# Gated DeltaNet on one core: another order of z, the convolutions, the inverse and the heads

## The chip, the core and the metric

The kernel runs on one core of a Trainium2 chip. The number is the device time of one execution in microseconds (us). Five engines work side by side, each through its own queue in order: PE (TensorE, matmuls and transposes; PEld is its weight load), DVE (VectorE), ACT (ScalarE), POOL (GpSimd) and SP (SyncE, which here issues the loads of weights). Operands lie in SBUF, PE writes to PSUM.

## The reference

Two layers on 256 tokens of 1024 numbers, all in float32. The change touches the mixer of the first layer, a gated DeltaNet with 8 heads of 128:

```python
x = x + 0.5 * swiglu(rmsnorm(x, ffn1_norm[layer]), ...)
x = x + mixer(rmsnorm(x, mix_norm[layer]))
x = x + 0.5 * swiglu(rmsnorm(x, ffn2_norm[layer]), ...)

proj = h @ w_in                      # q, k, v, z (1024 columns each), b, a
qkv = silu(causal_depthwise_conv(qkv, w_conv))        # 4 taps
q, k = l2norm(q) * DK ** -0.5, l2norm(k)
beta, g = sigmoid(b), -exp(A_log) * softplus(a + dt_bias)
# per head and chunk:
L = strictly_lower((k * beta) @ k.T * decay)
u, w = solve(I + L, [v * beta, k * beta * exp(g)])
o = (q * exp(g)) @ S + (q @ k.T * decay) @ (u - w @ S)
S = S * exp(g_last) + k_dec.T @ (u - w @ S)
y = (rmsnorm(o, out_norm) * silu(z)).reshape(T, H * DV) @ w_out
```

The kernel takes chunks of 128 tokens, so there are two chunks t = 0, 1. The second layer's mixer is a sliding-window attention and is not touched.

## The kernel before

**Matmuls.** Every large product of float32 numbers is done as three matmuls on parts: a weight piece `raw` of 128x1024 numbers is loaded by SP, ACT rounds it to a high part `whi` (L310), and DVE takes the low part `wlo` = raw - whi (L312), or POOL does it in four instructions of 128x256 (L317). `mm3` then makes hi x hi, hi x lo and lo x hi (L363 to L365).

**The mixer's stages** (about 195 to 370 us of the run). z, k, v and q are each projected in four chunks c of 256 columns. A chunk of z is 48 matmuls of 128x256 into PSUM buffers (`pz`, copied by ACT to `zs`). A chunk of k, v or q (`conv`) has two halves f of 128 columns: 24 matmuls `pcv` each, then ACT starts `cv` with one tap (L925), DVE adds three more from PSUM (L928), and ACT takes the silu (L932). PSUM has four buffers psA for pz, pcv and acc, four psB for the rest.

After each k chunk, `kpost` transposes k (`pkn`), sums its squares (L721) and makes k k^T (`pkk`), which DVE multiplies by the decay into `nf`. `blocks(g)` takes the 32x32 diagonal blocks of the four heads of group g, scales them by `knbr` and masks them on POOL (L768, L770). `inverse` inverts all these small triangles on DVE, from a transpose at L780 to one at L818, whose output is `yx`. `chain(g)` builds the full 128x128 inverse `yf` of each head and chunk from them, by small matmuls on PE with a copy by ACT or DVE behind each: `pt`, `py` (L833), `pt` (L853), `py` (L865), `px` (L873), `pt` (L881), `py` (L887). `state` then makes u, w and S (`puu`, `pwt`, `pS`, `pws`). `qpost` makes q k^T (`pkq`) and the squares of q (`pqn`) per q chunk. `o_of(t, g)` makes the outputs `po` of four heads, `post` normalises and gates them (ACT square L1051, DVE sum L1052, POOL power L1055, DVE product L1057 into `on`), `turn` transposes them (`poT`) and splits them into `oT` (L1068, L1069). `out_part` multiplies by w_out into `acc`, `out_add` adds to x; `after(t)` normalises x for the next FFN, whose transposes are `psT` and whose first products are `pgu`.

**The order.** The code is a program whose order is partly set by a `Ticker`: generators (gates, kpost, inverse, chain, state, ...) are advanced by one step after each f of a convolution. From that program a scheduler fixes each engine's order before the run, keeping an engine busy with what it thinks is ready, earlier code first; `issue_after` adds an order between two instructions. In the program before, z's chunks 0 to 2 come first, then k, v, q, with z's chunk 3 inside q's third; the inverse's steps and both chains go on one ticker.

Of the kernel before, what the change touches and what calls it, by code (L numbers as in the profile page):

```python
# [9 lines left out]
F32 = mybir.dt.float32  # L10
# [203 lines left out]
class Kern:  # L214
    def __init__(self, ctx, tc):
# [11 lines left out]
        self.early = None  # L227

# [59 lines left out]
    def split(self, src, hi, lo, shape, eng=None, cuts=1):  # L288
# [9 lines left out]
        with ExitStack() as behind:  # L298
# [14 lines left out]
            if eng is not None:  # L313

                r, h, l = (a.rearrange("p a b -> p (a b)").rearrange("p (n f) -> p n f", f=256) for a in (raw, hi, lo))
                for i in range(4):
                    eng.tensor_tensor(out=l[:, i], in0=r[:, i], in1=h[:, i].bitcast(F32), op=ALU.subtract)  # L317
# [10 lines left out]
    def wcols(self, w, c0, npool=0):  # L328
        src = w[:, c0:c0 + 256].rearrange("(k p) f -> p k f", p=P)
        pieces = [self.wpiece(src[:, 4 * i:4 * i + 4, :], 4, 256,  # L330
                              eng=self.nc.gpsimd if i >= 2 - npool else None) for i in range(2)]
        return lambda k, cs: tuple(a[:, k % 4, cs] for a in pieces[k // 4])
# [47 lines left out]
    def proj_T(self, out, w, f, nrm):  # L380
        fs = slice(f * P, (f + 1) * P)
        for k in range(KT):
            wh, wl = w(k, fs)
            self.mm3(out, wh, wl, nrm.h.hi(k), nrm.h.lo(k), k == 0, k == KT - 1)
# [217 lines left out]
    def gdn_gates(self, nrm, wh, wl, expA, dtb, Dt, wq, res):  # L602
# [27 lines left out]
        nc.scalar.activation(e, na, AF.Exp)  # L630
# [50 lines left out]
    def gdn(self, nrm, prep, w_in, w_out, after):  # L681
# [9 lines left out]
        tk = Ticker()  # L691
        Dt = self.big([P, NT, H, P], "Dt")
# [24 lines left out]
        def sumsq(pv, ss, h0):  # L717
            for i in range(2):
                for t in range(NT):
                    j = self.small([P, P], "junk", 1)  # L720
                    nc.scalar.activation(j, pv[:, t, i, :], AF.Square, accum_out=ss[:, t, h0 + i:h0 + i + 1])  # L721
# [3 lines left out]
        def kpost(c):  # L725
# [7 lines left out]
            beta, eG, eS = res["beta"], res["eG"], res["eS"]  # L733
# [7 lines left out]
            a = ssk[:, :, hs]  # L741
            nc.vector.tensor_scalar_add(a, a, EPS)
            nc.vector.reciprocal(br[:, :, hs], a)
            nc.vector.tensor_mul(br[:, :, hs], br[:, :, hs], beta[:, :, hs])
            nc.vector.tensor_scalar_mul(nbr[:, :, hs], br[:, :, hs], -1.0)
            yield
            nc.gpsimd.tensor_tensor(out=kd[:, hs, :], in0=kd[:, hs, :], in1=bc(eS, 0, hs), op=ALU.mult)
            nc.gpsimd.tensor_tensor(out=keg[:, hs, :], in0=keg[:, hs, :], in1=bc(eG, 1, hs), op=ALU.mult)
# [7 lines left out]
        def blocks(g):  # L756
# [4 lines left out]
            us = slice(8 * g, 8 * g + 8)  # L761
            raw = self.y1([P, 8, 32], "d32")
# [6 lines left out]
            for j, m in enumerate(("tri16", "off16")):  # L769
                nc.gpsimd.tensor_tensor(out=d2[:, j, us, :], in0=raw,  # L770
                                        in1=M[m].unsqueeze(1).to_broadcast([P, 8, 32]), op=ALU.mult)
            nc.gpsimd.tensor_tensor(out=sv[:, :, gs], in0=ssk[:, :, gs],
                                    in1=self.phalf.rearrange("p (t h) -> p t h", t=NT), op=ALU.pow)

        def inverse():
# [21 lines left out]
            yield  # L797
# [13 lines left out]
            yield  # L811
# [6 lines left out]
            nc.vector.transpose(yx[:, 1].rearrange("p u c -> p (u c)"), yx[:, 0].rearrange("p u c -> p (u c)"))  # L818
            late["yx"] = yx
            tk.add(chain(0), chain(1))  # L820

        def chain(g):
# [6 lines left out]
            def blockwise(ps, lhsT, rhs):  # L829
                for i in range(8):  # L830
                    for b in range(4):
                        bs = slice(32 * b, 32 * b + 32)
                        nc.tensor.matmul(ps[bs, i * 32:i * 32 + 32], lhsT=lhsT[bs, i, :], rhs=rhs[bs, i, :],  # L833
                                         start=True, stop=True)
# [540 lines left out]
```

## Time and profile before

| | us |
|---|---|
| median of three runs (lowest, highest) | 1017.47 (1017.03, 1020.1) |
| the profiled execution | 1017.73 |
| its span in the profile | 1016.0 |
| PE busy | 998.0 |

The profile is of one execution. A row of the waits names the engine and instruction that stood still, what released it, and the us. A row of a timeline has start, duration, engine, line, operation, output and inputs, and behind it in brackets the idle time ahead and its releaser. Groups of instructions have the count, busy us, mean ns, and idle us ahead. Windows give busy us of each engine in a stretch and the granted clock of PE (1.00 is full speed).

### The profile page before, as it was taken

To read this page: it belongs to the slowest core of one execution; us is meant where nothing else is said; L and a number is where in the kernel's file an instruction comes from. 1 tells how busy PE (TensorE), PEld (TensorE's weight loads), DVE (VectorE), ACT (ScalarE), POOL (GpSimd) and SP (SyncE) were. 2 spreads that over 40 slices of the span, in tenths; PEclk is the share of its full clock that TensorE was granted. 3 is DMA by queue.
4 is the path that set the end of the run, shared out by engine and by line. 5 is a ranking of instruction groups with operands and counts; after the bars stand their busy time and mean duration, and the time that the engine had idled before them with its cause. 6 is when DMAs were issued, how large, how long until landed. Compare 5 with 4: busy or idle time off the path is not lost.

```text
span 1016.0 us, 16483 instructions
## 1 busy us (share of the span) xinstructions
PE 998.0 (98%) x6195; PEld 870.7 (86%) x6195; DVE 643.7 (63%) x975; ACT 547.8 (54%) x979; POOL 242.1 (24%) x311
## 2 busy tenths in 40 slices
PE   8999999999989999999999999999999999999997
PEld 7888888899979888888888888888898678888886
DVE  5866654666895766666546666664578756666544
ACT  5756544457856445555434655553467545555442
POOL 0125510017952301323100123320021402222100
PEclk9999999999999999999999999999999999999999
DMA  7766666644452337666666666665563426666661
GB/s 246 235 188 191 200 197 182 205 129 148 133 175 65 105 104 208 195 188 197 191 199 190 186 187 186 192 207 189 185 209 104 152 91 212 190 189 187 203 188 43
DMA packets 135316, 177.05 MB, mean 174 GB/s; under 512 B 7250, under 2 KB 120260, under 8 KB 135236
## 3 DMA queue, kind: packets, MB, share of 16 engines
q1 hardware_dynamic: 132032, 171.46, 55.3%
q10 hardware_dynamic: 3204, 4.53, 1.4%
q8 instruction: 49, 0.80, 0.3%
q14 instruction: 31, 0.25, 0.1%
HBM read 174.92 MB, written 1.05 MB: 173 GB/s over the span
## 4 chain that ended last, share of the span: by engine, by line
PE 89%; DVE 4%; ACT 3%; issue 1%; DMA 1%; POOL 1%; SPq 1%; POOLq 0%; ACTq 0%
PE pg L370 14%; PE pu L370 14%; PE acc L365 9%; PE acc L363 9%; PE acc L364 9%; PE pu L371 7%; PE pg L371 7%; PE pgu L365 2%; PE pgu L364 2%; PE pgu L363 2%; DVE wlo L312 1%; DMA raw<-in_ffn_w_gu_dram 1%; PE pcv L363 1%; PE pcv L364 1%; PE pcv L365 1%
## 5 line engine op out<-in xcount | busy, mean ns | idle before, releaser
L312 DVE TENSOR_TENSOR wlo<-raw,whi 128x1024 fp32r<-128x1024 f32 (+1 forms) x304 | 374.9, 1236 | 198.0 <-ACT whi L310 196.8
L310 ACT CAST whi<-raw 128x1024 fp32r<-128x1024 f32 (+1 forms) x318 | 330.3, 1046 | 179.5 <-PE acc L365 83.2
L370 PE MATMUL pg<-hs,whi 128*128 128x512 f32 x624 | 218.7, 392 | 0.0
L370 PE MATMUL pu<-hs,whi 128*128 128x512 f32 x624 | 218.4, 392 | 0.0
L371 PE MATMUL pu<-hs,wlo 128*128 128x256 f32 x624 | 175.4, 281 | 0.0
L371 PE MATMUL pg<-hs,wlo 128*128 128x256 f32 x624 | 174.6, 281 | 0.0
L478 POOL TENSOR_TENSOR act<-act,gate 128x256 f32<-128x256 f32 x78 | 58.6, 751 | 352.0 <-DVE act L477 337.4
L370 PEld LDWEIGHTS pg<-hs,whi 128*128 128x128 f32 x624 | 116.9, 187 | 25.3
L370 PEld LDWEIGHTS pu<-hs,whi 128*128 128x128 f32 x624 | 116.9, 187 | 25.2
L364 PE MATMUL acc<-wlo,ah 128*128 128x512 f32 (+1 forms) x340 | 128.6, 378 | 0.0
L365 PE MATMUL acc<-whi,al 128*128 128x512 f32 (+1 forms) x340 | 128.5, 378 | 0.0
L363 PE MATMUL acc<-whi,ah 128*128 128x512 f32 (+1 forms) x340 | 128.0, 378 | 0.0
L371 PEld LDWEIGHTS pg<-hs,wlo 128*128 128x128 f32 x624 | 118.2, 189 | 0.4
L371 PEld LDWEIGHTS pu<-hs,wlo 128*128 128x128 f32 x624 | 118.2, 189 | 0.0
L363 PEld LDWEIGHTS acc<-whi,ah 128*128 128x128 f32 x340 | 64.0, 188 | 12.0
L364 PEld LDWEIGHTS acc<-wlo,ah 128*128 128x128 f32 x340 | 64.0, 188 | 11.8
L365 PEld LDWEIGHTS acc<-whi,al 128*128 128x128 f32 x340 | 64.0, 188 | 11.9
L481 POOL TENSOR_SCALAR ah<-act 128x256 fp32r<-128x256 f32 x78 | 66.4, 852 | 6.7
L467 ACT COPY gate<-pg 128x256 f32<-128x256 f32 x78 | 28.7, 368 | 55.6 <-PE pg L371 55.6
L476 ACT COPY act<-pu 128x256 f32<-128x256 f32 x78 | 28.7, 368 | 54.1 <-PE pu L371 54.1
L363 PE MATMUL pcv<-hs,whi 128*128 128x256 f32 x192 | 55.1, 287 | 2.2 <-DVE cv L928 2.2
L99 POOL TENSOR_TENSOR rst<-var,mhalf 128x1 f32<-128x1 f32 x10 | 5.6, 557 | 215.6 <-DVE var L97 215.6
(340 smaller groups left out, 1576.6 us busy)
## 6 DMA issues: line engine op xcount, KB each, us to landing
raw<-in_ffn_w_gu_dram SPq DMA_DIRECT2D x156, 512.0 KB, 4.4
raw<-in_ffn_w_down_dram SPq DMA_DIRECT2D x88, 512.0 KB, 4.2
raw<-in_a_w_in_dram SPq DMA_DIRECT2D x32, 512.0 KB, 4.2
raw<-in_ffn_w_gu_dram SPq DMA_DIRECT2D x40, 256.0 KB, 4.7
raw<-in_b_w_in_dram SPq DMA_DIRECT2D x12, 512.0 KB, 4.8
raw<-in_a_w_out_dram SPq DMA_DIRECT2D x8, 512.0 KB, 3.7
raw<-in_b_w_out_dram SPq DMA_DIRECT2D x8, 512.0 KB, 3.7
nw<-in_ffn_norm_dram ACTq DMA_DIRECT2D x3, 512.0 KB, 4.0
```

The source lines that it names most:

```text
L99: nc.gpsimd.tensor_tensor(out=r, in0=v, in1=k.mhalf[:, 0:1], op=ALU.pow)
L310: nc.scalar.copy(hi[:, c], raw[:, c])
L312: nc.vector.tensor_tensor(out=lo[:, c], in0=raw[:, c], in1=hi[:, c].bitcast(F32), op=ALU.subtract)
L363: nc.tensor.matmul(out, lhsT=lh, rhs=rh, start=start, stop=False)
L364: nc.tensor.matmul(out, lhsT=lh, rhs=rl, start=False, stop=False)
L365: return nc.tensor.matmul(out, lhsT=ll, rhs=rh, start=False, stop=stop)
L370: nc.tensor.matmul(out, lhsT=lh, rhs=r2, start=start, stop=False)
L371: return nc.tensor.matmul(out[:, :T], lhsT=ll, rhs=rh, start=False, stop=stop)
L467: nc.scalar.copy(g, pg[:, T:])
L476: nc.scalar.copy(a, pu[:, T:])
L478: nc.gpsimd.tensor_tensor(out=a, in0=a, in1=gates[f], op=ALU.mult)
L481: ahead[2] = nc.gpsimd.tensor_scalar(oh, a, 1.0, None, op0=ALU.mult)
```

## The change

z's chunks 2 and 3 move behind the k convolutions. A chunk of z and a convolution now have two PSUM accumulators open: the first four k pieces for both, then the last four for both. Each chain has a ticker of its own, advanced at every quarter of a convolution, and its matmuls are placed behind the matmuls of that quarter (`late["mm"]`). The inverse has no yields. The scaling of kd and keg goes behind the last POOL piece of v's second chunk. br and nbr are computed per group in `blocks`, the root of ssk in `roots`. Squares of k and q are one ACT instruction of 128x512 in place and one DVE sum. Of the weights of z's chunks 2 and 3 and of the k chunks 0 to 2, one piece of two gets its low part on POOL (before: none of z, 0, 0, 1, 1 for the k chunks). The outputs of heads 0 to 3 for both chunks, their post and turn come during q's convolutions (`heads`). At the end both chunks' acc are open, and the first four k pieces of both precede the turns of heads 4 to 7. z is gated in pieces of 128x256.

On DVE, the end of the inverse in the order before (cv are taps, wlo low parts of weights, yx the result):

```order
L810 TENSOR_REDUCE inv<-tw 128x8x8
L928 SCALAR_TENSOR_TENSOR cv<-pcv,wc,cv 128x255 x2
L812 COPY tw<-inv 128x512
L928 SCALAR_TENSOR_TENSOR cv<-pcv,wc,cv 128x254 x2
L815 STREAM_TRANSPOSE tw<-tw 128x16x32
L928 SCALAR_TENSOR_TENSOR cv<-pcv,wc,cv 128x253
L312 TENSOR_TENSOR wlo<-raw,whi 128x1024
L928 SCALAR_TENSOR_TENSOR cv<-pcv,wc,cv 128x253
L816 TENSOR_TENSOR yx<-tw,blk_953 128x512
L312 TENSOR_TENSOR wlo<-raw,whi 128x1024
L928 SCALAR_TENSOR_TENSOR cv<-pcv,wc,cv 128x255
L818 STREAM_TRANSPOSE yx<-yx 128x512
```

and after:

```order
L313 TENSOR_TENSOR wlo<-raw,whi 128x1024
L823 COPY tw<-inv 128x512
L951 SCALAR_TENSOR_TENSOR cv<-pcv,wc,cv 128x255
L951 SCALAR_TENSOR_TENSOR cv<-pcv,wc,cv 128x253
L826 STREAM_TRANSPOSE tw<-tw 128x16x32
L951 SCALAR_TENSOR_TENSOR cv<-pcv,wc,cv 128x254
L827 TENSOR_TENSOR yx<-tw,blk_953 128x512
L951 SCALAR_TENSOR_TENSOR cv<-pcv,wc,cv 128x255
L951 SCALAR_TENSOR_TENSOR cv<-pcv,wc,cv 128x253
L829 STREAM_TRANSPOSE yx<-yx 128x512
L951 SCALAR_TENSOR_TENSOR cv<-pcv,wc,cv 128x254
L313 TENSOR_TENSOR wlo<-raw,whi 128x1024
```

Low parts of weights stand thinner here; the taps alternate with the steps as before.

On POOL, the masked blocks ahead of the inverse, before (d are the blocks, kk the two scaled copies of k, ks the root of ssk):

```order
L770 TENSOR_TENSOR d_2607<-d_2608,tri_958 128x256
L770 TENSOR_TENSOR d_2607<-d_2608,off_967 128x256
L317 TENSOR_TENSOR wlo<-raw,whi 128x256 x4
L772 TENSOR_TENSOR ks<-ssk,phalf 128x2x4
L768 TENSOR_TENSOR d_2781<-d_2781,knbr 128x256
L770 TENSOR_TENSOR d_2607<-d_2781,tri_958 128x256
L770 TENSOR_TENSOR d_2607<-d_2781,off_967 128x256
L317 TENSOR_TENSOR wlo<-raw,whi 128x256 x12
```

and after, where the masks for the second group (d<-d,tri) are followed by the remaining scalings:

```order
L785 TENSOR_TENSOR ks<-ssk,phalf 128x2x4
L775 TENSOR_TENSOR d_2595<-d_2595,knbr 128x256
L318 TENSOR_TENSOR wlo<-raw,whi 128x256 x4
L747 TENSOR_TENSOR kk_1908<-kk_1908,gexp 128x256
L748 TENSOR_TENSOR kk_1908<-kk_1908,gexp 128x256
L747 TENSOR_TENSOR kk_1908<-kk_1908,gexp 128x256
L777 TENSOR_TENSOR d_2421<-d_2595,tri_958 128x256
L777 TENSOR_TENSOR d_2421<-d_2595,off_967 128x256
L785 TENSOR_TENSOR ks<-ssk,phalf 128x2x4
L748 TENSOR_TENSOR kk_1908<-kk_1908,gexp 128x256
```

One low part and now three scalings stand between d<-d,knbr and its masks; the root comes behind them.

On PE, what follows q's last convolution, before (py and puu are of chain and state, pkq and pqn of q):

```order
L365 MATMUL pcv<-hs,wlo 128x256
L887 MATMUL py<-yf,xa 64x64 x16
L1004 MATMUL puu<-u,yf 128x128 x8
L901 MATMUL pkq<-qT,kT 128x128 x4
L714 MATMUL pqn<-ident,qT 128x128 x4
L1004 MATMUL pwt<-yf,kk_1908 128x128 x8
L1004 MATMUL po<-u,Dt 128x128 x4
L1004 MATMUL pS<-u,kk_1908 128x128 x8
L901 MATMUL pkq<-qT,kT 128x128 x4
L714 MATMUL pqn<-ident,qT 128x128 x4
```

and after:

```order
L1039 MATMUL po<-S,wq 128x128
L1039 MATMUL po<-u,Dt 128x128
L917 MATMUL pkq<-qT,kT 128x128
L718 MATMUL pqn<-ident,qT 128x128 x2
L917 MATMUL pkq<-qT,kT 128x128 x3
L718 MATMUL pqn<-ident,qT 128x128 x2
L1103 MATMUL poT<-ident,on 128x128 x4
L365 MATMUL acc<-whi,oT 128x512
L366 MATMUL acc<-wlo,oT 128x512
```

The products of the chain and of the state that stood behind the last convolution are gone from there; po, pkq and pqn of the last q chunk and a poT are followed by acc.

```diff
-            for i in range(2):
-                for t in range(NT):
-                    j = self.small([P, P], "junk", 1)
-                    nc.scalar.activation(j, pv[:, t, i, :], AF.Square, accum_out=ss[:, t, h0 + i:h0 + i + 1])
+            nc.scalar.activation(pv, pv, AF.Square)
+            nc.vector.tensor_reduce(out=ss[:, :, h0:h0 + 2], in_=pv, axis=AX.X, op=ALU.add)
...
-            nc.scalar.copy(kd[:, hs, :], pv[:, 0])
-            nc.scalar.copy(keg[:, hs, :], pv[:, 1])
+            nc.scalar.copy(kk2[:, :, hs, :], pv)
...
-            nc.gpsimd.tensor_tensor(out=kd[:, hs, :], in0=kd[:, hs, :], in1=bc(eS, 0, hs), op=ALU.mult)
-            nc.gpsimd.tensor_tensor(out=keg[:, hs, :], in0=keg[:, hs, :], in1=bc(eG, 1, hs), op=ALU.mult)
+        def kscale():
+            eG, eS = res["eG"], res["eS"]
+            for c in range(4):
+                hs = slice(2 * c, 2 * c + 2)
+                with self.tc.issue_after(late["short"].ins):
+                    nc.gpsimd.tensor_tensor(out=kd[:, hs, :], in0=kd[:, hs, :], in1=bc(eS, 0, hs), op=ALU.mult)
+                    nc.gpsimd.tensor_tensor(out=keg[:, hs, :], in0=keg[:, hs, :], in1=bc(eG, 1, hs), op=ALU.mult)
+                yield
...
             late["yx"] = yx
-            tk.add(chain(0), chain(1))
...
+                with self.tc.issue_after(late["mm"].ins):
+                    for i in range(8):
...
-        def conv(col0, dst, npool, start):
+        def conv(col0, dst, npool, start, early=False):
             w = self.wcols(w_in, col0, npool)
-            for f in range(2):
-                ct = col0 // P + f
-                ps = self.psA("pcv")
-                self.proj_T(ps[:, :T], w, f, nrm)
...
+            acc = [self.psA("pcv") for f in range(2)]
+            for half in range(2):
+                for f in range(2):
+                    late["mm"] = self.proj_T(acc[f][:, :T], w, f, nrm, range(4 * half, 4 * half + 4))
+                    tkc[f].tick()
+                    if half:
+                        taps(col0 // P + f, acc[f], dst(f), early)
+                        tk.tick()
             tk.add(*start, first=True)
...
-        zmore(1)
         for c in range(4):
...
-            conv(D + c * 256, lambda f: kT[:, 2 * c + f, :], c // 2, [then(*steps)])
-            if c == 3:
-                tk.tick()
+            conv(D + c * 256, lambda f: kT[:, 2 * c + f, :], int(c < 3), [then(*steps)], early=c < 2)
+        tk.tick()
+        zmore(2)
...
+            if c == 0:
+                roots(1, late["d"])
+            if c == 1:
+                late["short"] = self.short
+                for g in range(2):
+                    tkc[g].add(chain(g))
+                tk.add(kscale())
...
-        def first():
-            o_of(0, 0)
-            post(0, 0)
-            yield
-            yield
-            turn(0, 0)
-            yield
+        def heads(g):
+            while "state" not in late:
+                yield
+            for t in range(NT):
+                o_of(t, g)
+                post(t, g)
+                yield
+            for t in range(NT):
+                yield
+                turn(t, g)
...
             if c == 1:
-                tk.add(then(first))
-            if c == 2:
-                n = 2 * zc[0]
-                w = self.wcols(w_in, 3 * D + 3 * 256)
-                for t in range(NT):
-                    zproj(3, t, w)
-                    zgate(t, slice(n, H))
-                    tk.tick()
-        tk.drain()
+                tk.add(heads(0))
+        for ticker in (*tkc, tk):
+            ticker.drain()
...
+        acc = [[self.psA("acc") for n in range(2)] for t in range(NT)]
+
+        def out(t, n, ks):
+            self.out_part(acc[t][n], ob[t], ws, n, ks)
+
+        for t in range(NT):
+            last = o_of(t, 1)
+
+            self.early = post(t, 1)
         for n in range(2):
-            self.out_part(acc[n], ob[0], ws, n, range(0, 4))
-        o_of(1, 1)
-
-        self.early = post(1, 1)
+            out(0, n, range(0, 4))
+        with self.tc.issue_after(last.ins):
+            for n in range(2):
+                out(1, n, range(0, 4))
         turn(0, 1)
-        turn(1, 0)
         for n in range(2):
-            self.out_part(acc[n], ob[0], ws, n, range(4, KT))
-            self.out_add(acc[n], 0, n)
+            out(0, n, range(4, KT))
+            self.out_add(acc[0][n], 0, n)
         turn(1, 1)
         after(0)
         for n in range(2):
-            a = self.psA("acc")
-            self.out_part(a, ob[1], ws, n, range(KT))
-            self.out_add(a, 1, n)
+            out(1, n, range(4, KT))
+            self.out_add(acc[1][n], 1, n)
         after(1)
```

More of the change, by code (lines that the diff above doesn't have):

```diff
@@ L378, in proj_T2, with proj_T @@
         return mm
-    def proj_T(self, out, w, f, nrm):
+    def proj_T(self, out, w, f, nrm, ks=range(KT)):
         fs = slice(f * P, (f + 1) * P)
-        for k in range(KT):
+        for k in ks:
             wh, wl = w(k, fs)
-            self.mm3(out, wh, wl, nrm.h.hi(k), nrm.h.lo(k), k == 0, k == KT - 1)
+            mm = self.mm3(out, wh, wl, nrm.h.hi(k), nrm.h.lo(k), k == 0, k == KT - 1)
+        return mm
     def proj_N(self, out, w, t, nrm):
@@ L691, in gdn @@
         tk = Ticker()
+        tkc = [Ticker() for g in range(2)]
         Dt = self.big([P, NT, H, P], "Dt")
@@ L769, in blocks, with roots @@
             for j, m in enumerate(("tri16", "off16")):
[L770 to L773, printed above, removed]
+                late["d"] = nc.gpsimd.tensor_tensor(out=d2[:, j, us, :], in0=raw,
+                                                    in1=M[m].unsqueeze(1).to_broadcast([P, 8, 32]), op=ALU.mult)
+            if g == 0:
+                roots(g, late["d"])
+        def roots(g, behind):
+            gs = slice(4 * g, 4 * g + 4)
+            with self.tc.issue_after(behind.ins):
+                nc.gpsimd.tensor_tensor(out=sv[:, :, gs], in0=ssk[:, :, gs],
+                                        in1=self.phalf.rearrange("p (t h) -> p t h", t=NT), op=ALU.pow)
         def inverse():
@@ L944, in zgate @@
             keep(nc.scalar.activation(z, z, AF.Silu))
-            keep(nc.gpsimd.tensor_tensor(
-                out=z, in0=z, in1=onb.unsqueeze(1).to_broadcast([P, hs.stop - hs.start, P]), op=ALU.mult))
+            for h in range(hs.start, hs.stop, 2):
+                z = zs[:, t, h:h + 2]
+                keep(nc.gpsimd.tensor_tensor(out=z, in0=z, in1=onb.unsqueeze(1).to_broadcast([P, 2, P]), op=ALU.mult))
         def zgates():
@@ L972, in zmore @@
             for c in range(zc[0], zc[0] + n):
-                w = self.wcols(w_in, 3 * D + c * 256)
-                for t in range(NT):
-                    zproj(c, t, w)
-                    tk.tick()
+                w = self.wcols(w_in, 3 * D + c * 256, 1)
+                acc = [self.psA("pz") for t in range(NT)]
+                for half in range(2):
+                    for t in range(NT):
+                        self.part_N(acc[t][:, :T], w, t, nrm.h, range(4 * half, 4 * half + 4))
+                        if half:
+                            zcopy(c, t, acc[t])
+                            tk.tick()
             zc[0] += n
-        zmore(1)
         for c in range(4):
@@ L1003, in mm @@
         def mm(out, lhsT, rhs, start=True, stop=True):
-            nc.tensor.matmul(out, lhsT=lhsT, rhs=rhs, start=start, stop=stop)
+            return nc.tensor.matmul(out, lhsT=lhsT, rhs=rhs, start=start, stop=stop)
         S = self.s4([P, H, P], "S")
@@ L1036, in state @@
                                                    in1=u[:, 1, h, :], op0=ALU.mult, op1=ALU.add)
+            late["state"] = True
             yield
```

79 lines of the change are left out of this document (40 added, 39 removed).

## The prediction

> **What bounds the kernel now.** I read the page first, then the waits of TensorE in the stretch that the change touches, then that stretch in windows of 5 us, then the timelines of the engines that TensorE waits for.
>
> ```profile
> span 1016.0 us, 16483 instructions
> PE 998.0 (98%) x6195; PEld 870.7 (86%) x6195; DVE 643.7 (63%) x975; ACT 547.8 (54%) x979; POOL 242.1 (24%) x311
> PE 89%; DVE 4%; ACT 3%; issue 1%; DMA 1%; POOL 1%; SPq 1%; POOLq 0%; ACTq 0%
> ```
>
> TensorE (PE) is busy for 98% of the span and carries 89% of the chain that ended last. The change leaves the set of matmuls as it is, so it can only win where PE stands still or runs slowly, and lose where it makes PE wait anew. The whole idle time in the mixer's second half, from 270 to 470 us, is this (us in total, times, longest):
>
> ```profile
> PE pcv L363 <- DVE cv L928: 2.2, 2, 1.5
> PE py L833 <- ACT t L837: 2.0, 1, 2.0
> PE acc L363 <- ACT oT L1068: 0.7, 1, 0.7
> PE pt L833 <- DVE yx L818: 0.5, 1, 0.5
> PE pt L853 <- DVE X L844: 0.5, 1, 0.5
> ```
>
> These are 5.9 us, and every one lies between 280 and 352 us. The windows (us, then busy us and count of PE, PEld, DVE, ACT, POOL; then the granted clock) show a second loss:
>
> ```profile
> 280.00:285.00 5.00, 3.50 (x30) 3.33 (x29) 5.00 (x12) 2.59 (x5) 3.75 (x5) 1.00 0.42 126
> 285.00:290.00 5.00, 5.00 (x42) 5.00 (x43) 5.00 (x10) 3.35 (x6) 0.85 (x1) 1.00 0.82 238
> 290.00:295.00 5.00, 4.30 (x36) 4.13 (x36) 5.00 (x7) 3.06 (x6) 2.92 (x2) 1.00 0.41 133
> 295.00:300.00 5.00, 4.04 (x150) 3.55 (x149) 5.00 (x8) 1.55 (x3) 4.52 (x7) 1.00 0.42 150
> 300.00:305.00 5.00, 3.49 (x136) 3.41 (x137) 4.53 (x13) 2.83 (x10) 1.60 (x2) 0.70 0.64 213
> 305.00:310.00 5.00, 4.53 (x90) 4.28 (x90) 3.70 (x8) 3.50 (x9) 0.74 (x1) 0.96 0.05 9
> 310.00:340.00 30.00, 30.00 (x340) 28.65 (x339) 17.45 (x39) 18.07 (x49) 10.29 (x12) 1.00 0.17 53
> ```
>
> In the two windows around 303 us the clock is 0.70 and 0.96: (0.30 + 0.04) x 5 us = 1.7 us of full-speed time lost, behind the 0.5 and 2.0 us waits at the chain's start. So 5.9 + 1.7 = 7.6 us is all that the rows let this change take away, out of 1017.73 us (span 1016.0 plus 1.73 around it). What can be told from no change here is 0.3%, or 3.05 us.
>
> **Why PE waits there.** In 280 to 300 us DVE (VectorE) has 5.00 of 5 us in each window. It carries the inverse, the taps of the convolutions (three per tile) and the low halves of the weights at once (count, busy us, mean ns; window 271.4 to 297.6):
>
> ```profile
> L928 DVE SCALAR_TENSOR_TENSOR cv<-pcv,wc,cv 128x255 f32<-128x255 f32 (+2 forms) x20 | 8.9, 465 | 0.0
> L312 DVE TENSOR_TENSOR wlo<-raw,whi 128x1024 fp32r<-128x1024 f32 x5 | 8.3, 1652 | 0.0
> ```
> ```profile
> 271.47 1.11 DVE L780 STREAM_TRANSPOSE tw<-d 128x512 f32<-128x512 f32 x1 [0.35 <-POOL d L770]
> ...
> 296.88 0.69 DVE L818 STREAM_TRANSPOSE yx<-yx 128x512 f32<-128x512 f32 x1
> ```
>
> From the first transpose to the last it is 297.57 - 271.47 = 26.1 us without a gap. A tap that comes late holds a PSUM buffer of psA (four of them), and the next pcv waits: the 1.5 and 0.7 us. The inverse's end releases the chain: the 0.5 us.
>
> **Term 1, the stretch up to the chain's start.** In the new order the inverse lies between 17 taps and 3 low halves instead of 19 and 5 (counted in the order between the same two transposes). Two taps at 0.465 and two low halves at 1.652 us less are 4.2 us: the inverse takes 26.1 - 4.2 = 21.9 us. Its start hangs on POOL (GpSimd), whose queue holds, ahead of the masked blocks that the first transpose reads, one low half of v and three scalings:
>
> ```profile
> 262.07 0.62 POOL L747 TENSOR_TENSOR kk<-kk,gexp 128x256 f32<-128x256 f32 x1
> 263.21 0.75 POOL L770 TENSOR_TENSOR d<-d,tri 128x256 f32<-128x256 f32 x1
> 264.61 2.84 POOL L317 TENSOR_TENSOR wlo<-raw,whi 128x256 fp32r<-128x256 f32 x4
> ```
> ```profile
> L765 ACT COPY d<-nf 32x256 f32<-32x256 f32 x8 | 3.2, 400 | 0.1
> ```
> ```profile
> 317.84 0.28 PE L363 MATMUL pcv<-hs,whi 128*128 128x256 f32 x1
> 317.96 0.28 PE L364 MATMUL pcv<-hs,whi 128*128 128x256 f32 x1
> ```
>
> On POOL that is 0.6 (d x knbr) + 2.8 + 3 x 0.6 + 0.7 = 5.9 us behind the last k blocks. Those are ready about 3.5 us after the last pkk (one DVE product, the reciprocals, four ACT copies of 0.4 us), which PE reaches at about 253 us (the matmuls ahead of it, 0.12 us from start to start, counted along the trace of before). So the first transpose comes at 253 + 3.5 + 5.9 = 262.4 us: 9 us earlier than before, but beside the convolutions of v, not beside z, since PE is done with z at 256 to 257. DVE then ends near 284.3. The tap that frees the psA buffer for q's second accumulator stands about 1 us ahead of that, at 283.3.
>
> PE without waits is at the chain 80 matmuls of 128x256 (9.6 us) and one group of four transposes (0.4) earlier than before: 297.6 - 2.7 of waits - 10.0 = 284.9, and 24 matmuls (2.9 us) ahead of it, at 282.0, at q's second accumulator. With the small start gaps that carry no idle mark I put it 0.9 earlier, at 281.1. It waits there 283.3 - 281.1 = 2.2 us, and no more at the chain itself (286.2 against 284.3). Before, the same stretch had 2.2 + 0.5 = 2.7. **Term 1: -0.5 us.** Bounds: if the inverse started 2.2 us earlier nothing would be left (-2.7); if it started 2 us later, or the low halves beside POOL took 2.87 us as here,
>
> ```profile
> 293.18 2.30 POOL L945 TENSOR_TENSOR zs<-zs,onb 128x768 f32<-128x768 f32 x1
> 293.69 2.87 DVE L312 TENSOR_TENSOR wlo<-raw,whi 128x1024 fp32r<-128x1024 f32 x1
> 299.03 1.26 DVE L312 TENSOR_TENSOR wlo<-raw,whi 128x1024 fp32r<-128x1024 f32 x1
> ```
>
> the wait would be up to 4.2 (+1.5). The change sends three more pieces of weights to POOL in four parts each, 3 x 2.84 = 8.5 us there for 3 x 1.26 saved on DVE. On POOL itself nothing of it is late but the chain just costed.
>
> Against this speaks the Trainium skill, SBUF — State Buffer, "Who interferes with whom": a VectorE instruction with both inputs in SBUF contends with GpSimd instructions that read SBUF, one with a single SBUF input does not. The low half is of the first kind and a tap (PSUM and SBUF) of the second; the 2.87 against 1.26 us above agrees. By that rule all three low halves beside the inverse would be slow ones and term 1 would end near its upper bound, a sum of about 2 us more.
>
> **Term 2, inside the chain.** The chain's first steps were 2.0 (py, on ACT's copy t) and 0.5 (pt, on DVE's X):
>
> ```profile
> 300.78 0.42 ACT L932 ACTIVATE qT<-cv 128x256 f32<-128x256 f32 x1 [1.16 <-DVE cv L928]
> 301.10 0.63 ACT L837 COPY t<-pt 128x256 f32<-128x256 f32 x2
> ```
>
> The copy stood in ACT's queue behind a silu that waited for taps. In the new order it stands behind one conv copy, one cast of weights and one silu instead (about 0.8 us of wait); two matmuls and later four pcv (0.5 us) lie between the steps where DVE needs about 1.5 for Y and X (1.0); and px waits for ACT's copies behind a silu of 128x1024 (0.9). 2.7 against 2.5: **term 2: +0.2 us**, bounds -1.5 (the copies find ACT free) and +1.5 (each of the two stalls as long as the 2.0 of before). All later steps of the chain, the state and the first half of the heads get 156 matmuls of q's convolutions as cover (18.7 us), which they did not have; before, 310 to 340 us showed no idle PE either, so that is worth nothing.
>
> **Term 3, the clock.** A wait of 1.5 us at 283 left the clock at 1.00, the 0.5 and 2.0 together did not. The new ones are 2.2 us alone, then 0.8 to 1.0 with work between them. I take it that the clock holds. **Term 3: -1.7 us**, bounds -1.7 and 0 (at the first stall of 2.2 as easily as before at 2.0).
>
> **Term 4, the tail.** Before, 15 us of small matmuls and half of the output projection lay between q's last convolution and the products that need it. Now only one group of po (8 matmuls) does, and both halves of the projection come behind. Rows of before for the latencies:
>
> ```profile
> 344.69 1.27 ACT L1051 ACTIVATE on<-po 128x512 f32<-128x512 f32 x2 [2.97 <-PE po L1004]
> 345.32 1.36 DVE L1052 TENSOR_REDUCE so<-on 128x4 f32<-128x512 f32 x2 [1.67 <-ACT on L1051]
> 346.82 1.98 POOL L1055 TENSOR_TENSOR fo<-fo,mhalf 128x4 f32<-128x4 f32 x2 [5.53 <-DVE fo L1054]
> 347.86 2.16 DVE L1057 SCALAR_TENSOR_TENSOR on<-po,fo,zs 128x128 f32<-128x128 f32 x8 [0.99 <-POOL fo L1055]
> 351.06 0.50 PE L363 MATMUL acc<-whi,oT 128*128 128x512 f32 x1 [0.65 <-ACT oT L1068]
> 363.47 0.39 PE L365 MATMUL acc<-whi,oT 128*128 128x512 f32 x1
> 363.70 0.39 PE L363 MATMUL acc<-whi,oT 128*128 128x512 f32 x1
> 366.21 1.08 ACT L115 CAST hs<-psT 128x512 fp32r<-128x512 f32 x2 [3.48 <-PE psT L112]
> ```
>
> pkq waits for q's last head: conv copy 0.5, three taps 1.3, silu 0.4 are 2.2 us behind the last pcv against 1.8 us of po: 0.4, or 0.75 if ACT does the squares of po (0.6) first. The first acc stands right behind its own transposes: 0.65 as in the row above, or 1.2 with the low half. The second poT group: 0 to 0.25. Acc behind poT of the other heads: 0.65 to 0.8. The last poT waits on post (0.6 + 0.7 + 1.0 + 1.1 = 3.4 us from squares to on) behind 24 acc of 0.23 us from start to start (5.5): 0, or 1.35 if two low halves of weights stand ahead on DVE. psT is no longer followed by eleven acc but by pgu, which needs the 0.6 us cast: 0.4 to 0.7. Sum 2.1 to 5.05; I take the middle, 3.6. Before there were 0.7 at acc and about 1.0 in unmarked gaps at the same places (the second psT had no cover either). **Term 4: +1.9 us**, bounds +0.4 and +3.4.
>
> **The rest, at nothing.** The wide squares take 16 pairs of ACT instructions of each kind away and add 8 ACT squares and 8 DVE sums; pkn's share alone:
>
> ```profile
> L721 ACT ACTIVATE junk<-pkn 128x128 f32<-128x128 f32 x16 | 4.6, 284 | 0.2
> L721 ACT ACTIVATION_READ_ACCUMULATOR junk<-pkn 128x1 f32 x16 | 3.4, 210 | 0.0
> ```
>
> ACT gains some 10 us of 547.8 and DVE gets 8 x 0.7. Both lie under PE's matmuls, outside the 21.9 us; without that cover each DVE sum costs 0.7 us where it lands. The joined kd/keg copies, the later kd/keg scaling, the gathered br/nbr and the halves of zs x onb hide in the same way. The order of the weights' transfers on SP does not change, so DMAs cost nothing new. Two accumulators per convolution use the same four buffers; what they cost is in term 1.
>
> **Sum.** -0.5 + 0.2 - 1.7 + 1.9 = -0.1 us on 1017.73: 1017.6; the profiled execution is 0.26 above the median of the three runs shown, so **1017.4 us**.
>
> **Rivals.** *The stalls do go away* (chance 0.32): DVE's work beside the inverse is lighter by more than I count, term 1 is -2.7, term 2 -1.5, the clock -1.7 and the tail +0.9: -5.0, 1012.5 us. For it: 4 us less work in DVE's window and chains spread over quarters. Against it: the inverse still falls on v's taps. *The tail turns into the bound* (0.25): from q's last pcv on, each step is a round trip through ACT and DVE with casts of weights between them; all waits at their upper end are +3.4, and 0.75 + 1.2 within a few us are enough to halve the clock once there (3.4 us at half speed, +1.7), with terms 1 and 2 at +0.7: -1.7 + 3.4 + 1.7 + 0.7 = +4.1, 1021.6 us. It decides from 3 us of new idle between the last pcv and pgu. *The change does not do what it says*: the inverse stays beside convolutions and term 1 alone falls to 0; that is 0.5 us and lies inside the forecast.
>
> On the clock, the Trainium skill, TensorE: Matmul & The Clock Gate, "What's actually happening", has a free-running window of 3413 ns; the 1.7 us lost here are 3.4 us at half speed and agree in length. Whether a given 2 us stall halves it would then hang on the window's phase, which no run here shows yet.
>
> **How the numbers follow.** Forecast 0.43, the two rivals 0.32 and 0.25. The forecast's own spread is the four bounds, mostly within 3 us of 1017.4; the 8-in-10 range reaches into both rivals, 1012.4 to 1021.6. Faster by over 0.3% needs -3.05 us, which is the first rival; slower the second.
>
> **What would show it.** Right: the first transpose of the inverse at 261 to 264 us and about 22 us to the last; a wait of pcv on cv of 1 to 3 us; no window under 0.95 of the clock from 280 to 310; waits of pkq, acc and poT of 2 to 5 us in sum between q's last pcv and FFN's first pgu. Wrong: the inverse beside pz, no pcv wait at all, or a window of half clock in the tail.

## The result: 1029.0 us against 1017.5, slower by 1.0%

The changed kernel took 1028.99 us (median of 4, 1028.06 to 1030.87), the kernel before 1017.50 in the same comparison: a ratio of 1.0102 (95% interval 1.0081 to 1.0122), or 10.4 us more. The profiled executions, 1028.06 and 1017.73 us, differ by 10.3. From the mixer's first pz to the first pg of the next FFN the one takes 193.98 us (195.15 to 389.13), the other 183.80 (195.39 to 379.19): 10.2 of it arise in the mixer.

The waits of PE from 195 to 480 us in the profile after (us in total, times, longest):

```profile
PE pcv L365 <- DVE cv L951: 3.9, 2, 2.4
PE acc L365 <- ACT oT L1106: 2.7, 2, 2.0
PE py L845 <- issue: 2.0, 1, 2.0
PE poT L1103 <- DVE on L1095: 0.9, 1, 0.9
PE pvn L718 <- ACT vT L956: 0.8, 1, 0.8
PE pkq L917 <- ACT qT L956: 0.6, 1, 0.6
PE pt L866 <- issue: 0.4, 1, 0.4
PE pgu L365 <- ACT hs L115: 0.3, 1, 0.3
PE pab L365 <- ACT hs L115: 0.2, 1, 0.2
```

Without pab, which is the same in both, they are 11.6 us against 5.9: 5.7 more. The rest is the clock. In windows cut where it changes, the profile after has (us; busy us and count of PE, PEld, DVE, ACT, POOL; granted clock):

```profile
281.00:284.30 3.30, 1.06 (x9) 0.85 (x8) 3.30 (x5) 0.44 (x2) 3.30 (x4) 1.00 0.42 132
284.30:287.70 3.40, 3.29 (x15) 3.32 (x16) 3.40 (x7) 2.14 (x4) 2.94 (x4) 0.50 0.79 244
291.20:294.60 3.40, 1.43 (x98) 1.15 (x89) 0.52 (x2) 1.64 (x6) 2.77 (x4) 0.99 0.26 101
294.60:298.00 3.40, 3.40 (x106) 2.94 (x96) 2.72 (x9) 1.14 (x4) 0.00 (x0) 0.50 0.55 159
359.40:362.80 3.40, 1.32 (x6) 0.55 (x4) 2.71 (x7) 1.88 (x2) 2.09 (x2) 1.00 0.87 238
362.80:369.60 6.80, 6.06 (x16) 4.91 (x17) 4.68 (x8) 2.33 (x4) 0.47 (x1) 0.50 0.92 300
```

Each of the three places with long stalls (2.4 us before a pcv, 2.0 in py, 0.9 and 2.0 in the tail) is followed by a stretch at half clock: 3.4, 3.4 and 6.8 us, where before there was one of 3.4. In these stretches PE is busy 3.29 + 3.40 + 6.06 = 12.75 us, before 3.40. Half of that is lost: 6.4 us against 1.7, or 4.7 more. PE's busy time in the mixer grew by the same 4.7 (182.26 us instead of 177.56) and its idle time by 5.5 (the listed waits have 5.7); together they are the 10.2.

My theory after this reading: three separate causes, each with a stall of about 2 us and a half-clock stretch behind it. In front, POOL is full beside the inverse; in the chain, PE's instructions come too late; in the tail, ACT's queue holds casts that wait for transfers, ahead of the cast that acc needs. The rivals stand with each experiment. Ratios below are against the kernel before in the same comparison, with 95% intervals; 0.001 is 1.02 us.

### The profile page after: what moved, and what is told of

It is laid out like the page before. It is cut to its first block, busy times and chain, and to the rows that moved or that the text cites. A ratio compares the mean times of both kernels' runs of the same rounds, so it can differ in the third digit from the quotient of the medians.

```text
span 1026.3 us, 16436 instructions
## 1 busy us (share of the span) xinstructions
PE 1002.6 (98%) x6195; PEld 873.0 (85%) x6195; DVE 644.7 (63%) x972; ACT 545.4 (53%) x919; POOL 252.9 (25%) x327
## 4 chain that ended last, share of the span: by engine, by line
PE 89%; ACT 3%; POOL 2%; DVE 2%; issue 2%; DMA 1%; SPq 0%; POOLq 0%; ACTq 0%; DVEq 0%
PE pg L372 14%; PE pu L372 14%; PE acc L365 9%; PE acc L367 9%; PE acc L366 9%; PE pu L373 7%; PE pg L373 7%; PE pgu L367 2%; PE pgu L366 2%; PE pgu L365 2%; PE pcv L365 1%; PE pcv L366 1%; PE pcv L367 1%; POOL wlo L318 1%; DMA raw<-in_ffn_w_gu_dram 1%
## 5 line engine op out<-in xcount | busy, mean ns | idle before, releaser
L313 DVE TENSOR_TENSOR wlo<-raw,whi 128x1024 fp32r<-128x1024 f32 (+1 forms) x301 | 369.8, 1232 | 199.4 <-ACT whi L311 194.5
L366 PEld LDWEIGHTS acc<-wlo,ah 128*128 128x128 f32 x340 | 64.0, 188 | 11.6
L318 POOL TENSOR_TENSOR wlo<-raw,whi 128x256 fp32r<-128x256 f32 x68 | 58.6, 894 | 36.0 <-ACT whi L311 34.4
```

The costliest lines, as they stand in the source:

```text
L313: nc.vector.tensor_tensor(out=lo[:, c], in0=raw[:, c], in1=hi[:, c].bitcast(F32), op=ALU.subtract)
L318: self.short = eng.tensor_tensor(out=l[:, i], in0=r[:, i], in1=h[:, i].bitcast(F32), op=ALU.subtract)
L366: nc.tensor.matmul(out, lhsT=lh, rhs=rl, start=False, stop=False)
```

## The experiments

### The tail: ACT's queue

In the profile after, ACT has these rows (start, us, and in brackets the idle time ahead); SP's issues of the next FFN's weights start at 355.73:

```profile
344.70 0.59 ACT L1106 CAST oT<-poT 128x512 fp32r<-128x512 f32 x1
351.59 0.58 ACT L1106 CAST oT<-poT 128x512 fp32r<-128x512 f32 x1 [6.30 <-PE poT L1103]
352.07 1.99 ACT L311 CAST whi<-raw 128x1024 fp32r<-128x1024 f32 x2
...
359.61 1.04 ACT L311 CAST whi<-raw 128x1024 fp32r<-128x1024 f32 x1 [2.66 <-DMA raw<-in_ffn_w_gu_dram]
361.96 1.04 ACT L311 CAST whi<-raw 128x1024 fp32r<-128x1024 f32 x1 [1.31 <-DMA raw<-in_ffn_w_gu_dram]
362.91 0.58 ACT L1106 CAST oT<-poT 128x512 fp32r<-128x512 f32 x1
```
```profile
355.73 6.14 SPq L296 DMA_DIRECT2D raw<-in_ffn_w_gu_dram  x8
```

The second oT cast waits 6.3 us for a poT that stands behind 24 acc. Four casts of w_out wait behind it and hold the four raw buffers; so the next FFN's weights are asked for at 355.7, their casts wait for them in ACT's queue, and the oT cast for which PE stands comes only at 362.9.

**The next FFN's casts behind the last turn.**

```diff
-            self.early = post(t, 1)
+            post(t, 1)
...
-        turn(1, 1)
+        self.early = turn(1, 1)
```

> The changed kernel, with the three ACT casts of the next FFN's weights placed behind the cast of the last turn instead of behind the last square. Queue theory (acc waited 2.0 us because oT's cast stood in ACT's queue behind casts that waited for transfers, and the clock then halved for two windows): the wait of acc on oT falls from 2.0 to 0.8 us or less, at most one half-clock window is left behind 340 us, and the time falls by 3 to 5.5 us from 1028. Latency rival (each step from post to acc is a round trip that the covers are too short for, whatever stands in the queue): the wait of acc on oT stays above 1.5 us and the time within 1.5 us of 1028.

Measured: 1.0117 (1.009 to 1.0144), no faster than the change. The long wait did go, and the tail's half-clock stretch shrank from 6.8 to 3.4 us in the profiled execution. But three waits of up to 0.7 (2.1 us in sum) stand at acc instead, and a new one of 1.4 at psT, since DVE's norm now stood behind three late low halves (3.50 us). My theory missed the time: these casts alone, moved back, hand the lateness on. The rival's time came true, its long wait did not.

**One turn later**, so that w_out's casts come ahead of it.

```diff
-            for t in range(NT):
-                yield
-                turn(t, g)
+            yield
+            turn(0, g)
...
+        turn(1, 0)
         with self.tc.issue_after(last.ins):
```

> The changed kernel, with the turn of heads 0 to 3 of the second chunk moved from q's convolutions to behind the first half of the projection, so that ACT's casts of w_out come ahead of that oT. Queue theory: ACT no longer stands 6.3 us with four casts behind it, the raw buffers come free near 345 instead of 352 to 356 us, the transfers of the next FFN's weights are issued 5 us or more earlier, no cast there waits for a transfer by over 0.5 us, and the time falls by 3 to 6 us from 1028. Latency rival: transfers come earlier too, but acc still waits 1.5 us or more on oT and the time stays within 1.5 us of 1028.

Measured: 1.0052 (1.0031 to 1.0073), 5.1 us less than the change. The profile is of the slowest of its six executions (1026.75 us, median 1022.59). In the tail there is left, in the same view of the waits (340 to 390 us):

```profile
PE acc L365 <- ACT oT L1106: 0.7, 1, 0.7
PE pkq L917 <- ACT qT L956: 0.5, 1, 0.5
PE po L1039 <- DVE Dt L918: 0.3, 1, 0.3
PE pgu L365 <- ACT hs L115: 0.3, 1, 0.3
```

No half clock is left in the tail. The transfers are issued at 351.42, 4.3 us earlier (5 was expected). One cast still waits 2.8 us for its transfer, against the expectation, but two oT casts follow right behind it, ahead of the next two.

**The change's tail alone**, on the kernel before, and the same with the one turn moved:

```diff
+        def heads(g):
...
-                tk.add(then(first))
+                tk.add(heads(0))
...
+        acc = [[self.psA("acc") for n in range(2)] for t in range(NT)]
...
```

> The kernel before with the change's heads and tail alone (both chunks of heads 0 to 3 and their turns early, four acc open), everything ahead of them as before. Queue theory: ACT's queue has the same order as in the changed kernel (two oT casts ahead of the casts of w_out), so the same wait of about 2 us of acc on oT, late transfers of the next FFN's weights and mostly a half-clock stretch come with it: 4 to 8 us slower than 1018. Rival (the tail was only bad because the front had made it late): within 2 us of 1018.

> The same with the one turn of the second chunk behind the first half of the projection. Queue theory: the casts of w_out come ahead of that turn, the wait of acc on oT is 1 us or less, and it is 4 us or more faster than the change's tail alone; against the kernel before from -1 to +3 us. Rival (tail bad for its short covers): no more than 2 us faster than the change's tail alone.

Measured: 1.0070 (1.0058 to 1.0083) and 1.0036 (1.0024 to 1.0048). The tail alone shows the same picture: acc waits 2.0 us, the second oT stands 6.07, a half-clock stretch follows, and the time is 7.1 us longer. So the front didn't make it late. Moving the turn takes 3.5 us off, less than the 4 expected and more than the rival's 2: poT still waits 1.7 us for DVE in both. So about half of the tail's price is the queue. Of the other half, 3.7 us, 2.0 are waits in the tail (poT 1.7, po 0.4, acc 0.3 and pgu 0.3, against 0.7 at acc before), round trips of the kind that the latency rival named; the rest is not located.

### The front: POOL beside the inverse

DVE's products in the inverse (lines 805 and 808 before, 817 and 820 after), first before, then after, and after's taps and low halves in the stretch of the inverse:

```profile
279.28 0.42 DVE L805 TENSOR_TENSOR tw<-inv 128x64 f32<-128x64 f32 x2
282.00 1.05 DVE L805 TENSOR_TENSOR tw<-inv 128x512 f32<-128x512 f32 x1
285.12 1.12 DVE L808 TENSOR_TENSOR tw<-iw,inv 128x512 f32<-128x512 f32 x1
```
```profile
270.82 1.14 DVE L817 TENSOR_TENSOR tw<-inv 128x64 f32<-128x64 f32 x2
275.68 1.04 DVE L817 TENSOR_TENSOR tw<-inv 128x512 f32<-128x512 f32 x1
278.00 1.58 DVE L820 TENSOR_TENSOR tw<-iw,inv 128x512 f32<-128x512 f32 x1
```
```profile
L951 DVE SCALAR_TENSOR_TENSOR cv<-pcv,wc,cv 128x253 f32<-128x253 f32 (+2 forms) x18 | 8.1, 459 | 0.0
L313 DVE TENSOR_TENSOR wlo<-raw,whi 128x1024 fp32r<-128x1024 f32 x3 | 4.7, 1556 | 0.0
```

On POOL, after, in the same stretch, and the inverse's first transpose on DVE:

```profile
257.94 0.61 POOL L775 TENSOR_TENSOR d<-d,knbr 128x256 f32<-128x256 f32 x1
258.51 3.82 POOL L318 TENSOR_TENSOR wlo<-raw,whi 128x256 fp32r<-128x256 f32 x4
...
270.45 15.01 POOL L318 TENSOR_TENSOR wlo<-raw,whi 128x256 fp32r<-128x256 f32 x16
```
```profile
264.77 1.07 DVE L793 STREAM_TRANSPOSE tw<-d 128x512 f32<-128x512 f32 x1 [3.12 <-POOL d L777]
```

The pair of 128x64 products, with both inputs in SBUF, grew from 0.42 to 1.14 us while POOL worked without a break, and the last 128x512 product from 1.12 to 1.58. The first 128x512 product stayed at 1.04, and the taps, with one input in PSUM, at 0.46. All the inverse's own steps together took 13.4 us instead of 12.6. POOL's pieces have the same median of 0.74 us and the same longest of 1.72 in both stretches. The Trainium skill, SBUF — State Buffer, "Who interferes with whom", has a VectorE instruction with two SBUF inputs contend with a GpSimd instruction that reads SBUF. The slower products and the unchanged taps agree with it; the first 128x512 product shows that not each one is slower.

> The changed kernel with POOL's share of the low halves as before the change (k chunks 0, 0, 1, 1; none of z). POOL theory (POOL is full from 250 to 285 us, which delays the masked blocks and slows DVE's two-input instructions beside it): the inverse's first transpose comes 3 us or more earlier, the waits of pcv on cv fall from 3.9 to 2 us or less and no half-clock window follows them; the time falls by 3 to 6 us. DVE-count rival (every low half that POOL doesn't take is 1.2 us more on the engine that is the limit): three more low halves on DVE, the waits of pcv stay at 3.5 us or grow, the time stays or rises by up to 3 us.

```diff
-                w = self.wcols(w_in, 3 * D + c * 256, 1)
+                w = self.wcols(w_in, 3 * D + c * 256)
...
-            conv(D + c * 256, ..., int(c < 3), [then(*steps)], early=c < 2)
+            conv(D + c * 256, ..., c // 2, [then(*steps)], early=c < 2)
```

Measured: 1.0087 (1.0063 to 1.0111), which alone can't be told from the change. But the first transpose comes at 258.8, 6 us earlier, 11 taps stand in the inverse instead of 17, and pcv waits 1.8 us instead of 3.9, once, with no half clock. That profile is of the fastest of its four executions (1021.96 us, median 1025.73). What moved is the start: the masks follow d x knbr at once, where the change has 3.82 us of low half and 1.8 of scalings between. The products stayed slow (the pair at line 817 1.17 us, the last one 1.54), and the inverse still took 22.2 us although six taps fewer stood in it; so this run tests POOL's place ahead of the masks, not its work beside the products. Part of the gain comes back elsewhere: pkn waits 1.9 us for ACT (silu of k, the gates' exponentials) and pvn 1.3. With the tail's repair on top:

> The changed kernel with both repairs: POOL's share of the low halves as before the change, and the turn of heads 0 to 3 of the second chunk behind the first half of the projection. If the two causes (POOL beside the inverse, ACT's casts in the tail) are separate, their gains add: 3.3 and 6.4 us off 1029.0, so 1019.3 (1017.5 to 1021), waits of acc on oT 1 us or less, pcv on cv 2 us or less, no half clock in most executions. If they are one cause (the tail was only late because the front was), the second repair brings nothing more: 1022 to 1026.

Measured: 1.0025 (1.0016 to 1.0033), 7.8 us less than the change and inside the range for two separate causes. The turn's part is clear in time: 5.1 us from the change, and 6.3 from the kernel with POOL's share as before to this one. The rest, 2.7, is the part of POOL's share, but the intervals with the turn alone overlap a little, so in time it is likely and not shown. What is left against the kernel before shows in this profile as 8.0 us of waits instead of 5.9, with the same 3.4 us of half clock.

**Which pieces of POOL's, and z's place:** one piece of each of z's two chunks on POOL but k's as before; and z's third chunk ahead of k again.

> The changed kernel with the turn moved, POOL's share of k as before (0, 0, 1, 1), but one piece of each of z's chunks still on POOL. Tells which of POOL's extra pieces cost: the inverse starts as early in the order as with all of POOL's share as before (11 taps). If the pieces of k chunks 0 to 2 were the cause, 1021 (1019 to 1022.5), as with both repairs; if z's pieces were, pcv waits 3 us or more and the time is 1023 or more.

> As the kernel with both repairs, but z's third chunk stands ahead of the k convolutions again and only the fourth behind them. With k ahead of half of z, pkn waited for ACT's silu of k and its exponentials of the gates (1.9 us in the run with POOL's share as before). Theory: with z's third chunk ahead these waits go (under 0.5 us), but the inverse falls beside v's convolutions again, 19 taps instead of 11, and pcv waits for cv 2.5 us or more. Net within 2 us of the kernel with both repairs. Rival (the place of z is what costs the time): waits of both kinds under 1 us and a time at least 2 us under it.

Measured: 1.0033 (1.0022 to 1.0044) and 1.0019 (1.0011 to 1.0028). The first can't be told from both repairs, and its first transpose comes as early (258.7, 11 taps), so it is k's pieces on POOL and not z's that hold the inverse's start. The second isn't told apart either, which the theory allowed: the wait for ACT's exponentials went from 0.9 to 0.3 (that for the silu stayed at 1.0, against the theory), and pcv waited 3.7 us instead of 1.8.

**The early silu.** The change also lets the silu of k chunks 0 and 1 run ahead of the gates' exponentials. Free for all four chunks, and then for none (without and with k's pieces on POOL):

> The changed kernel with both repairs, and the silu of all four k chunks free to run ahead of the gates' exponentials (before: of the first two). Theory: the 1.9 us in which pkn waits for ACT's silu of k and the exponentials fall to 1 us or less and the time to 1019 to 1020, at best that of the kernel before. Rival (each change between silu and exponential costs ACT a load of its table, 1.3 us): ACT gets later, pkn waits 2 us or more, the time rises by 1 to 3 us over 1021.

> The changed kernel with POOL's share of k as before and the turn moved, and without the early silu of k chunks 0 and 1 (all silu behind the gates' exponentials again, so two loads of ACT's table, 2.6 us, less). Theory: the table loads were part of why pkn and pvn waited (0.7 and 2.1 us in the run with the early silu); without them these waits fall under 1.5 us in sum, the chain starts no later, and the time is 1016.5 to 1019, level with the kernel before or up to 1 us under it. Rival (the early silu feeds pkn and is needed): pkn waits 2 us or more, 1021 or more.

> The same with the change's share of POOL (one piece of each k chunk 0 to 2 there). Tells what POOL's share does apart from the table loads. POOL theory: the inverse stands beside 20 taps of v instead of 11, pcv waits 3 us or more for cv, 1021 to 1024. Rival (the table loads alone made the inverse late): within 1 us of the other kernel of this pair.

Measured: 1.0083 (1.007 to 1.0096), 1.0066 (1.005 to 1.0081) and 1.0070 (1.0054 to 1.0086). The first two are slower than the same kernels with the change's two chunks free (1.0025 and 1.0033); the third can't be told from its own (1.0052). For all four the rival was right: two loads of ACT's table more, and pkn waits 3.9 us; the time rose by 5.9, more than the rival's 1 to 3. For none, the edit did not do what I took it to do: one silu of k still runs between the exponentials, and ACT's groups show four loads as before the edit (here without k's pieces on POOL),

```profile
L956 ACT ACT_TABLE_LOAD x2 | 2.6, 1283 | 0.0
L627 ACT ACT_TABLE_LOAD x1 | 1.3, 1283 | 0.0
L681 ACT ACT_TABLE_LOAD x1 | 1.3, 1283 | 0.0
```

and pkn waits 2.5 us for k. So what the loads cost is not tested. The pair is also within 0.5 us of each other though pcv and pz wait for DVE's taps 1.6 us without k's pieces on POOL and 4.3 with them: the cheaper front was lost at pkn (2.5), pvn (1.3) and the clock (10.2 us of half clock against 6.8). Here POOL's share made no difference in time.

### The chain: instructions of PE

> The changed kernel with the second chain started one convolution later, so that 32 pt are followed by 24 pcv instead of 64 pt by 2 pcv and 64 py. Supply theory (the 2.0 us of py in which PE waits for nothing that the profile shows are PE's instructions not yet fetched, since small matmuls use them up faster): that idle in py disappears or falls under 0.5 us at the first chain. Copy rival (it is ACT's copy t after all): py still stands about 2 us behind pt. The time is no test here: the second chain and the state lose their cover behind q's last convolution, which should cost 5 to 12 us over the changed kernel.

```diff
             if c == 1:
                 late["short"] = self.short
-                for g in range(2):
-                    tkc[g].add(chain(g))
+                tkc[0].add(chain(0))
...
             if c == 0:
+                tkc[1].add(chain(1))
                 tk.add(state())
```

PE after the change, and the instruction queue's transfers from 291.7 to 293.1 us (packets, MB, share); in the 5.7 us ahead of that this queue moved nothing:

```profile
292.02 0.45 PE L845 MATMUL py<-yx,t 32*32 32x32 f32 x30
294.43 0.67 PE L845 MATMUL py<-yx,t 32*32 32x32 f32 x34 [1.97 <-issue]
```
```profile
q8 instruction: 1, 0.02, 5.2%
```

Measured: with 24 pcv between them, 64 pt and 64 py each run through in 0.75 us, and no idle "issue" is left in the first chain; the time is 1.0152 (1.0136 to 1.0169), 5.1 us more than the change, the low end of what the lost cover behind q's last convolution was to cost. Since 24 pcv (2.9 us) would also hide a late copy, this run alone doesn't settle it against the rival. The trace after the change does: ACT's copy t ended at 291.95, before the first py at 292.02, and PE stopped in the middle of the 64 py that read it. So the copy rival falls. In the three kernels with the same order of PE up to here (the change, and the two with only the tail changed) PE stopped after the same 30 of 64 py, for 1.8 to 2.3 us, each time 0.4 to 0.7 us behind the start of such a transfer. In the kernel before, one ran while PE waited for t anyway. That it is the supply of instructions fits all of these; it was not isolated further.

### Parts that were to cost nothing

On the kernel before, wide squares and the joined copy alone; and these with the late scaling and the split roots:

```diff
+            nc.scalar.activation(pv, pv, AF.Square)
+            nc.vector.tensor_reduce(out=ss[:, :, h0:h0 + 2], in_=pv, axis=AX.X, op=ALU.add)
...
```

> The kernel before, with one part of the change alone: wide squares (one ACT square and one DVE sum per chunk of k and q) and the joined copy of kd and keg. Theory of the prediction (this part costs nothing, PE's matmuls cover it): within 2 us of 1017.5. Since ACT and POOL's order move with it, the chain starts 24 matmuls earlier in PE's order and only 4 low halves stand in the inverse: if DVE is what delays the chain, the wait before the chain falls by up to 2 us. Rival (the DVE sums on the engine that is the limit delay it): waits of pcv and pt from 2.7 to 4 us and a time 1.5 to 4 us longer.

> The kernel before with wide squares, the late scaling of kd and keg and the split roots, but z, the convolutions, POOL's share, the heads and the tail as before. Theory: what made the change slow lies in z's place, POOL's share and the tail, so this kernel is within 2 us of 1017.5, or up to 3 us faster if the waits around the chain (5.2 us before) get shorter. Rival (late scaling makes POOL's queue late for state's products): pwt or pS waits for kk, 1 us or more, and a time 1 to 4 us longer.

Measured: 1.0007 (0.9998 to 1.0017) and 1.0022 (1.0012 to 1.0032). The first is no difference, as forecast, though its waits moved (one of 3.2 us at pcv instead of 1.5 and 0.7, py 1.5 instead of 2.0). The second is 2.2 us slower, a little more than the theory allowed. No wait of pwt or pS for kk stands in its list, so the rival named the wrong place: it has the 3.2 us at pcv and 1.9 us of "issue" in py.

No version beat the kernel before.

## Why the prediction was wrong

**Term 1 (-0.5 us) failed in size and sign.** PE's place was right: 290.34, where the chain began, less 3.9 + 0.8 of waits and 1.6 for the half clock is 284.0, the place forecast without waits, and the wait for a tap was of the kind named, 2.4 us against 2.2, though it stood 36 matmuls ahead of the chain, at q's first accumulator, not 24. But the same happened at the accumulator before it (1.6 us), and pvn waited 0.8: 4.7 in place of the 2.2 forecast, so +2.0 against before's 2.7. Three prices were taken too low. The first transpose came at 264.8, not 262.4: POOL's low half ahead of the masks was taken at 2.84 us and took 3.82, as another row of before had it (257.73); and 1.4 us were taken at nothing, because the last blocks were ready at 256.4 but POOL reached them at 257.94, behind the first group's masks and root (1.65). The inverse was taken at 21.9 us and took 22.7, since only taps and low halves were counted off, not that its own products would slow beside POOL. The "about 2 us more" that I had put aside, worked out from the rule of the Trainium skill, SBUF — State Buffer, "Who interferes with whom", came nearer by luck: it rested on three slow low halves, and these took 1.56 us on average, no more than the 1.65 of before.

**Term 2 (+0.2) was right in size for the wrong reason:** 2.4 us instead of 2.7 (-0.1 against before's 2.5), but none of it ACT's or DVE's copies; it was "issue".

**Term 3 (-1.7) is the step that failed most.** I took it that the clock holds with stalls of 2.2 us and would save the 1.7. It fell three times and cost 4.7 more than before. The row I leaned on, 1.5 us without a fall at 283 us, is one case: PE was busy 1.96 of 3.4 us in that window, and an idle of 2.2 us within one window leaves only 1.2. The prediction's own sign of being wrong, a window of half clock in the tail, came.

**Term 4 (+1.9) had the right place and too small a size.** 4.5 us of waits instead of 3.6, and +3.8 against the 0.7 of before. Its largest, 2.0 at acc, was listed with 0.65 to 0.8, as a latency. What was left out is that a cast at the head of ACT's queue holds raw buffers, and so delays transfers, and these then hold the queue.

**The measured sum:** +2.0 - 0.1 + 4.7 + 3.8 = +10.4 us, where the prediction had -0.1.

**At nothing:** the wide squares do cost nothing alone. The early silu was not costed at all: ACT's table loads went from 2 to 4. What these cost stays open, since no run took them away.

**The rivals.** The tail as the bound came closest, 1021.6; it counted one half-clock stretch of 3.4 us in the tail and none in front. That waits of 0.75 and 1.2 us would be enough to halve the clock there, no row of before showed; in the run with the casts behind the turn, 0.9 and 0.7 were. That the inverse does not get beside z was true, but was priced at 0.5 us. The range ended at this rival's 1021.6, which holds the tail at its bound and terms 1 and 2 at +0.7 together; here terms 1, 3 and 4 all went over their own upper bounds (+1.5, 0 and +3.4).

## What to carry to other kernels

A stall on the engine that is the limit can have two prices where its clock follows its load: its length, and half of the 3.4 or 6.8 us behind it; a stall of 2 us can be worth 3.7. Before moving a step, read the queue of each engine for what stands behind it, transfers and the buffers they need included: one copy that waited 6.3 us for PE held four casts, four buffers and the next stage's loads. Work given to POOL is not free for DVE where both read two operands from SBUF, and POOL's own queue can hold a step for which DVE waits.

## What the runs showed of the hardware

The clock goes by windows of 3.4 us: in the profile after it changes at 284.32, 287.73, 294.56, 297.97, 362.83 and 369.65 us, all on one grid of 3.41. PE need not be idle in a window for the next to run at half speed. The same stall of 1.76 us, in the run with both repairs and in that with POOL's share alone (the window ahead and the window behind):

```profile
272.50:275.90 3.40, 1.64 (x14) 1.44 (x13) 3.40 (x7) 0.95 (x2) 3.40 (x5) 1.00 0.70 192
276.00:279.30 3.30, 3.30 (x18) 3.30 (x17) 3.30 (x6) 2.80 (x8) 2.17 (x3) 0.50 0.35 119
```
```profile
271.20:274.60 3.40, 1.69 (x15) 1.49 (x13) 3.40 (x7) 0.00 (x0) 3.40 (x4) 1.00 0.51 151
274.70:278.00 3.30, 3.30 (x28) 3.30 (x29) 3.30 (x6) 2.81 (x8) 3.21 (x5) 1.00 0.57 160
```

PE was busy 1.64 of 3.4 us in the one, 1.69 in the other. In the sixteen traces, of the windows in which PE ran the large products alone, those with less than 1.6 us busy were followed by a fall and those with more than 1.7 were not: there the border lies close to half, and a stall of 1.5 to 2 us can fall on either side. Where 32x32 matmuls or transposes fill part of the window, the busy time does not tell: one with 2.3 us was followed by a fall (295.3 to 298.7 us in the run with the silu of all four chunks free), one with 1.8 was not (339.5 to 342.9 in the run with POOL's share alone). The time of one kernel spreads with it: the six executions with the one turn moved run from 1020.2 (mean clock 0.997) to 1026.8 us (0.992). The Trainium skill, TensorE: Matmul & The Clock Gate, "What's actually happening", has a free-running window of 3413 ns, with which these lengths agree, and a fall after an idle window; here a window that was half busy was enough, and the measurement decides.

A burst of small matmuls can be followed by a stop: 128 and then 30 of 32x32 from 290.34 to 292.47 us, then 2.0 us in which PE waited for nothing that the profile shows. Late instructions fit this and were not isolated. And the load of an ACT table took 1283 ns each time, as the Trainium skill, ScalarE activation tables: per-element evaluation and per-set limits, "What a function is on this engine", has it between functions of different sets.
